# The first 16 rows of a DMA-fed row sum in two transfers, one row and then 15, ahead of the opening barrier

## Chip, cores, metric

One core of one Trainium2 chip. The time is device microseconds (us) of one execution; several executions of each kernel are compared, and the profile is one of them.

## The reference

```python
def reference(x):                      # x: (32, 512, 1024) float32
    relu_x = np.maximum(x, 0)
    return np.sum(relu_x, axis=-1).astype(np.float32)      # (32, 512)
```

16384 rows of 4 KB are read once, 67.1 MB, and 64 KB are written. There is no reuse: the kernel is a stream from HBM with a small sum behind it.

## The kernel before

Each of 128 partitions handles 128 rows. The first 112 rows of a partition come in seven chunks of 16 rows (8 MB, 64 KB contiguous per partition) into three buffers; the last 16 rows come in ever smaller transfers. ScalarE applies the relu in place and VectorE sums; in the last chunk and the tail each engine does whole rows by itself. The opening barrier is the place at the program's start where the engines wait for one another; a load that SyncE issues ahead of it goes out at 0.00 us. Where packets are spoken of, "engine" means one of the 16 DMA engines, and in the profile SPq is SyncE issuing a transfer.

```python
REGIONS = [112, 16]
CHUNKS = [(0, 0), (0, 16), (0, 32), (0, 48), (0, 64), (0, 80), (0, 96)]
ACT_STEPS = [[7, 9], [7, 9], [4, 5, 7], [4, 5, 7], [4, 5, 7], [3, 4, 5]]
DVE_STEPS = [[7, 9], [7, 4, 5], [4, 5, 7], [4, 5, 7], [4, 5, 7], [3, 4, 5]]
TAIL = [8, 4, 2, 1]
# ... (cut)
    code = nc.main_func.blocks[0].instructions
    arrival = next(i for i, ins in enumerate(code)      # SyncE's arrival at the opening barrier
        if ins.engine == mybir.EngineType.SP and type(ins).__name__ == "InstDrain")
    for c in range(NBIG + 1):
        if c >= NB:
            sp.wait_ge(s_dve, done[c - NB])             # buffer free
        if c < NBIG:
            g, j = CHUNKS[c]
            sp.dma_start(out=buf[:, c % NB, :, :],
                         in_=xv[g][:, j : j + BIG, :]).then_inc(s_in[c], 16)
        if c == 0:
            code.insert(arrival, code.pop())            # the first load goes ahead of the barrier
# ... (cut: tail loads, stores)
    for c in range(NTWO):
        act.wait_ge(s_in[c], 16)
        for n in ACT_STEPS[c]:
            t = buf[:, c % NB, r : r + n, :]
            act.activation(t, t, AF.Relu).then_inc(s_act, 1)
        for n in DVE_STEPS[c]:
            # ... wait for s_act
            dve.tensor_reduce(out=res[...], in_=buf[:, c % NB, r : r + n, :],
                              axis=X, op=ALU.add).then_inc(s_dve, 1)
# ... (cut: last chunk, tail, closing store)
```

Of the kernel before, what the change touches and what calls it, by code (L numbers as in the profile page):

```python
# [5 lines left out]
BIG = 16  # L6
NB = 3
REGIONS = [112, 16]
CHUNKS = [(0, 0), (0, 16), (0, 32), (0, 48), (0, 64), (0, 80), (0, 96)]
ACT_STEPS = [[7, 9], [7, 9], [4, 5, 7], [4, 5, 7], [4, 5, 7], [3, 4, 5]]  # L10
DVE_STEPS = [[7, 9], [7, 4, 5], [4, 5, 7], [4, 5, 7], [4, 5, 7], [3, 4, 5]]
TAIL = [8, 4, 2, 1]
# [3 lines left out]
def bass_relu_sum_kernel(  # L16
# [17 lines left out]
    J = B * S // P  # L34
    NBIG = len(CHUNKS)
    assert BIG * NBIG + sum(TAIL) + 1 == J == sum(REGIONS) and sum(LAST) == D
# [4 lines left out]
    xv = [  # L41
        xr[P * s : P * (s + n), :].rearrange("(p j) d -> p j d", p=P)
        for s, n in zip(start, REGIONS)
    ]
    ov = [of[P * s : P * (s + n)].rearrange("(p j) -> p j", p=P) for s, n in zip(start, REGIONS)]

    buf = nc.alloc_sbuf_tensor("buf", [P, NB, BIG, D], fp32)
# [5 lines left out]
    s_in = [nc.alloc_semaphore(f"s_in{i}") for i in range(n_in)]  # L53
# [10 lines left out]
    sp, act, dve = nc.sync, nc.scalar, nc.vector  # L64
# [8 lines left out]
    code = nc.main_func.blocks[0].instructions  # L73
    arrival = next(
        i
        for i, ins in enumerate(code)
        if ins.engine == mybir.EngineType.SP and type(ins).__name__ == "InstDrain"
    )
    for c in range(NBIG + 1):
        if c >= NB:  # L80
            sp.wait_ge(s_dve, done[c - NB])
        if c < NBIG:
            g, j = CHUNKS[c]
            sp.dma_start(out=buf[:, c % NB, :, :], in_=xv[g][:, j : j + BIG, :]).then_inc(
                s_in[c], 16
            )
        if c == 0:
            code.insert(arrival, code.pop())
    r = 0
    tail = []  # L90
    for i, n in enumerate(TAIL):
# [13 lines left out]
    for g in range(len(REGIONS) - 1):  # L105
        sp.dma_start(
            out=ov[g][:, :], in_=res[:, start[g] : start[g] + REGIONS[g]]
# [3 lines left out]
    def on_act(t, acc):  # L111
        return act.activation(t, t, AF.Relu, accum_out=acc)  # L112

    def on_dve(t, acc):
        return dve.tensor_scalar(  # L115
            out=t, in0=t, scalar1=0.0, scalar2=None, op0=ALU.max, op1=ALU.add, accum_out=acc
        )

    def row(c, i):
        return buf[:, c % NB, i, :], res[:, c * BIG + i : c * BIG + i + 1]  # L120

    k = 0
    for c in range(NTWO):
        alone = BIG - sum(ACT_STEPS[c])
        act.wait_ge(s_in[c], 16)
        r = 0
        ready = []
        for n in ACT_STEPS[c]:
            t = buf[:, c % NB, r : r + n, :]
            act.activation(t, t, AF.Relu).then_inc(s_act, 1)  # L130
            k += 1
            ready += [k] * n
            r += n
        for i in range(BIG - alone // 2, BIG):
            on_act(*row(c, i))
        if alone:
            dve.wait_ge(s_in[c], 16)
            for i in range(BIG - alone, BIG - alone // 2):
                on_dve(*row(c, i))
        r = seen = 0  # L140
        for n in DVE_STEPS[c]:
            if ready[r + n - 1] > seen:
                seen = ready[r + n - 1]
                dve.wait_ge(s_act, seen)
            dve.tensor_reduce(  # L145
                out=res[:, c * BIG + r : c * BIG + r + n],
                in_=buf[:, c % NB, r : r + n, :],
                axis=X,
                op=ALU.add,
            ).then_inc(s_dve, 1)  # L150
            r += n
# [1 line left out]

    j0 = NBIG * BIG
    for c in range(NTWO, NBIG):
        act.wait_ge(s_in[c], 16)
        dve.wait_ge(s_in[c], 16)
        for i in range(BIG):
            ins = (on_act if i % 2 else on_dve)(*row(c, i))
            if i >= BIG - 2:  # L160
                ins.then_inc(s_fact if i % 2 else s_fdve, 1)
    for r, n, s in tail[:-1]:
# [13 lines left out]
        out=res[:, j0 + r : j0 + r + 1], in0=half[:, 0:1], in1=half[:, 1:2], op=ALU.add  # L176
    )

    n = LAST[2]
# [41 lines left out]
```

## Time and profile before

| | before |
|---|---|
| time, median of 3 (range) | 161.19 us (161.11 to 161.30) |
| span of the profile | 159.8 us |
| HBM read / written | 67.11 MB / 0.07 MB |
| input queue, share of 16 engines | 98.0% |
| VectorE / ScalarE busy | 121.4 / 101.5 us |
| landing of chunks 1, 2 and of the last input | 21.82, 41.18, 157.75 us |

The landings are the moments at which the last of a transfer's 16 semaphore increments arrives. The prediction below shows the lines that matter. Two things help in reading it. In rate rows and windows a DMA packet counts where it *starts*, with all its bytes, so short windows swing. And the trace keeps a record of each packet (start, duration, size), which shows starts and gaps that no row shows.

### The profile page before, as it was taken

The numbers are of one execution on the slowest core, as the hardware profiler recorded it, in microseconds if no ns is written. First come the engines' busy times: TensorE is split into PE (matmuls) and PEld (weight loads), VectorE is DVE, ScalarE is ACT, GpSimd is POOL, SyncE is SP. The second block draws the span as 40 slices with busy tenths as digits, with TensorE's granted clock in tenths as the row PEclk, the third lists the DMA queues.
The fourth block names the chain that finished last, engine by engine and source line by source line (L and its number), as shares of the span: only waits on it lengthen the run. The fifth ranks groups of instructions, "written<-read, shape, count | busy, mean of one in ns | idle before, by whom it ended". The sixth has DMA issues, their size and how long they took to land.

```text
span 159.8 us, 148 instructions
## 1 busy us (share of the span) xinstructions
DVE 121.4 (76%) x58; ACT 101.5 (63%) x55; POOL 0.2 (0%) x4
## 2 busy tenths in 40 slices
DVE  0000000999959999999969989699899999598995
ACT  3000059990699808996099951999339980496974
POOL 0000000000000000000000000000000000000000
DMA  7996996996997998989969969969969969899994
GB/s 262 525 525 262 525 525 262 525 525 262 525 443 344 525 410 377 525 361 427 525 295 492 525 279 509 525 262 525 525 262 525 525 262 525 353 435 394 406 393 138
DMA packets 2305, 67.18 MB, mean 420 GB/s; under 512 B 512, under 2 KB 768, under 8 KB 1024
## 3 DMA queue, kind: packets, MB, share of 16 engines
q1 hardware_dynamic: 2304, 67.18, 98.0%
q14 instruction: 1, 0.01, 0.0%
HBM read 67.11 MB, written 0.07 MB: 420 GB/s over the span
## 4 chain that ended last, share of the span: by engine, by line
DMA 68%; ACT 18%; DVE 11%; SPq 1%; issue 0%
DMA buf<-in_x_dram 68%; ACT buf L130 18%; DVE res L145 11%; SPq L92 1%; SPq L100 0%; DVE buf L115 0%; DVE last L115 0%
## 5 line engine op out<-in xcount | busy, mean ns | idle before, releaser
L145 DVE TENSOR_REDUCE res<-buf 128x7 f32<-128x7168 f32 (+4 forms) x17 | 100.1, 5923 | 34.0 <-ACT buf L130 34.0
L130 ACT ACTIVATE buf<-buf 128x7168 f32<-128x7168 f32 (+4 forms) x16 | 80.7, 5099 | 46.5 <-DMA buf<-in_x_dram 46.5
L112 ACT ACTIVATE buf<-buf 128x1024 f32<-128x1024 f32 (+1 forms) x19 | 19.0, 1000 | 9.0 <-DMA buf<-in_x_dram 8.9
L115 DVE TENSOR_SCALAR_CACHE_REDUCE buf<-buf 128x1024 f32<-128x1024 f32 (+2 forms) x19 | 20.9, 1146 | 2.8 <-DMA buf<-in_x_dram 2.5
L112 ACT ACTIVATION_READ_ACCUMULATOR buf<-buf 128x1 f32 x19 | 3.5, 186 | 0.0
L130 ACT ACT_TABLE_LOAD x1 | 1.3, 1283 | 0.8 <-PEq L206 0.8
L115 DVE DVE_READ_ACCUMULATOR buf<-buf 128x1 f32 x19 | 1.6, 83 | 0.0
L115 DVE TENSOR_SCALAR_CACHE_REDUCE last<-last 128x258 f32<-128x258 f32 x1 | 0.4, 422 | 0.0
L175 DVE TENSOR_TENSOR res<-half 128x1 f32<-128x1 f32 x1 | 0.2, 160 | 0.1
L206 POOL MEMSET const-bfloat16-1.0<- 128x1 bf16 x1 | 0.1, 101 | 0.0
L206 POOL MEMSET const-uint8-127<- 128x1 uint8 x1 | 0.1, 101 | 0.0
L206 POOL MEMSET const-float32-0.0<- 128x1 f32 x1 | 0.1, 98 | 0.2 <-issue 0.2
L206 POOL MEMSET const-float32-1.0<- 128x1 f32 x1 | 0.1, 98 | 0.0
L115 DVE DVE_READ_ACCUMULATOR last<-last 128x1 f32 x1 | 0.1, 81 | 0.0
## 6 DMA issues: line engine op xcount, KB each, us to landing
buf<-in_x_dram SPq DMA_DIRECT2D x1, 4096.0 KB, 26.7
buf<-in_x_dram SPq DMA_DIRECT2D x1, 2048.0 KB, 31.2
buf<-in_x_dram SPq DMA_DIRECT2D x1, 1024.0 KB, 33.2
buf<-in_x_dram SPq DMA_DIRECT2D x1, 512.0 KB, 34.0
buf<-in_x_dram SPq DMA_DIRECT2D x1, 256.0 KB, 34.2
buf<-in_x_dram SPq DMA_DIRECT2D x1, 128.0 KB, 34.1
last<-in_x_dram SPq DMA_DIRECT2D x1, 128.0 KB, 34.0
buf<-in_x_dram SPq DMA_DIRECT2D x7, 36.3
```

The lines of the kernel that those rows point to most:

```text
L92: sp.dma_start(out=buf[:, tb, r : r + n, :], in_=xv[-1][:, r : r + n, :]).then_inc(s_in[NBIG + i], 16)
L112: return act.activation(t, t, AF.Relu, accum_out=acc)
L115: return dve.tensor_scalar(out=t, in0=t, scalar1=0.0, scalar2=None, op0=ALU.max, op1=ALU.add, accum_out=acc)
L130: act.activation(t, t, AF.Relu).then_inc(s_act, 1)
L145: dve.tensor_reduce(out=res[:, c * BIG + r : c * BIG + r + n], in_=buf[:, c % NB, r : r + n, :], axis=X, op=ALU.add,).then_inc(s_dve, 1)
L175: dve.tensor_tensor(out=res[:, j0 + r : j0 + r + 1], in0=half[:, 0:1], in1=half[:, 1:2], op=ALU.add)
L206: nc = _bacc.Bacc("TRN2", target_bir_lowering=False, num_devices=1)
```

## The change

The intent is to let the stream start with small packets, so that the DMA engines have data flowing sooner, and to have the bulk queued right behind them. Both transfers count on one semaphore, and the waits ask for the sum of 32.

```diff
-CHUNKS = [(0, 0), (0, 16), (0, 32), (0, 48), (0, 64), (0, 80), (0, 96)]
+CHUNKS = [[(0, 0, 1), (0, 1, 15)]] + [[(0, 16 * c + 16, 16)] for c in range(6)]
@@
-            g, j = CHUNKS[c]
-            sp.dma_start(out=buf[:, c % NB, :, :], in_=xv[g][:, j : j + BIG, :]).then_inc(
-                s_in[c], 16
-            )
-        if c == 0:
-            code.insert(arrival, code.pop())
+            i = 0
+            for g, j, n in CHUNKS[c]:
+                sp.dma_start(
+                    out=buf[:, c % NB, i : i + n, :], in_=xv[g][:, j : j + n, :]
+                ).then_inc(s_in[c], 16)
+                i += n
+                if c == 0:
+                    code.insert(arrival, code.pop())
+                    arrival += 1
@@ every wait for a chunk, on ScalarE and VectorE
-        act.wait_ge(s_in[c], 16)
+        act.wait_ge(s_in[c], 16 * len(CHUNKS[c]))
```

More of the change, by code (lines that the diff above doesn't have):

```diff
@@ L136, in bass_relu_sum_kernel @@
         if alone:
-            dve.wait_ge(s_in[c], 16)
+            dve.wait_ge(s_in[c], 16 * len(CHUNKS[c]))
             for i in range(BIG - alone, BIG - alone // 2):
@@ L155, in bass_relu_sum_kernel @@
     for c in range(NTWO, NBIG):
-        act.wait_ge(s_in[c], 16)
-        dve.wait_ge(s_in[c], 16)
+        act.wait_ge(s_in[c], 16 * len(CHUNKS[c]))
+        dve.wait_ge(s_in[c], 16 * len(CHUNKS[c]))
         for i in range(BIG):
```

## The prediction

> **What bounds the kernel now.** I read the page first, then the waits, the SyncE queue's own waits, the timeline of the start and the end, and last the trace's record of single DMA packets. From the page:
>
> ```profile
> span 159.8 us, 148 instructions
> DVE 121.4 (76%) x58; ACT 101.5 (63%) x55; POOL 0.2 (0%) x4
> ...
> DVE  0000000999959999999969989699899999598995
> ACT  3000059990699808996099951999339980496974
> ...
> GB/s 262 525 525 262 525 525 262 525 525 262 525 443 344 525 410 377 525 361 427 525 295 492 525 279 509 525 262 525 525 262 525 525 262 525 353 435 394 406 393 138
> ...
> q1 hardware_dynamic: 2304, 67.18, 98.0%
> ...
> DMA 68%; ACT 18%; DVE 11%; SPq 1%; issue 0%
> ```
>
> No compute engine is full, and the one input queue is busy for 98% of 16 engines' span. The swing of the rate row between 262 and 525 is not a stall. A slice is 4 us and a packet counts where it starts. The packet records show 896 packets of 65536 B, each 2.418 us long and starting 2.416 us after the one before it on its engine, so a slice catches one or two starts per engine (16 x 65536 B / 4.0 us = 262 GB/s). The true rate is 16 x 65536 B / 2.416 us = 434 GB/s, with no hole from the second packet of an engine to the tail.
>
> The waits say who is short of what:
>
> ```profile
> ACT buf L130 <- DMA buf<-in_x_dram: 46.5, 6, 19.8
> DVE res L145 <- ACT buf L130: 34.0, 8, 28.1
> ...
> SPq L84 <- DVE res L145: 99.0, 4, 44.0
> ```
>
> ScalarE waits for a landing before each of the six pipelined chunks. VectorE in turn waits for ScalarE, mostly while nothing has arrived. SyncE waits 99.0 us for buffers, which looks like a bound; the timeline shows it isn't:
>
> ```profile
> 0.00 1.60 SPq L84 DMA_DIRECT2D buf<-in_x_dram  x3
> ...
> 0.79 1.28 ACT L130 ACT_TABLE_LOAD   x1 [0.79 <-PEq L206]
> 21.84 13.95 ACT L130 ACTIVATE buf<-buf 128x7168 f32<-128x7168 f32 x2 [19.77 <-DMA buf<-in_x_dram]
> ...
> 35.82 9.75 DVE L145 TENSOR_REDUCE res<-buf 128x9 f32<-128x9216 f32 x1 [0.15 <-ACT buf L130]
> 41.20 13.95 ACT L130 ACTIVATE buf<-buf 128x7168 f32<-128x7168 f32 x2 [5.41 <-DMA buf<-in_x_dram]
> 45.60 0.33 SPq L84 DMA_DIRECT2D buf<-in_x_dram  x1
> ```
>
> VectorE frees the first buffer at 35.82 + 9.75 = 45.57 us and the fourth chunk is issued at 45.60. The third chunk's packets run to about 60 us, so that issue is some 14 us early. Chunks land every 19.36 us (21.84 to 41.20), that is 8 packets x 2.416 = 19.33 us and 0.03 us for the change of transfer. So the end is set by three things in a row: when the stream starts, 64 rows of 64 KB per engine at 2.416 us (154.6 us), and what follows the last input. The last part is fixed:
>
> ```profile
> 157.88 0.42 DVE L115 TENSOR_SCALAR_CACHE_REDUCE last<-last 128x258 f32<-128x258 f32 x1
> ...
> 158.33 0.34 SPq L190 DMA_DIRECT2D out_dram<-res  x1
> ```
>
> The last input is there at 157.8, the store is issued at 158.33 and lands 1.4 us later, at the end of the span.
>
> The change touches only the first term. There the packet records show: issue at 0.00, first packets of the 16 engines starting between 1.00 and 1.86, ending between 4.07 and 4.53, so 2.6 to 3.5 us long (mean 3.08) in place of 2.42. Counted back from the ends by one full packet, the stream began to flow at 4.07 - 2.42 = 1.65 to 4.53 - 2.42 = 2.11 us. An engine keeps its place to the end, so the slowest engine's 2.11 us is the whole stake of this change, less the issue-to-first-packet time that no splitting removes.
>
> **What the Trainium skill says.** (1) "DMA: Bandwidth & Descriptors", section "Where 436 GB/s comes from", gives a ceiling of 435.2 GB/s for the 16 ports; the trace's 434 agrees, so nothing can make up for a late start. (2) The same page, "Latency and other measured facts", gives about 0.6 us to the first byte for a transfer issued from SyncE and a round trip to HBM of at least about 0.8 us, whatever the size. The trace has 0.84 us from the issue of the closing store to its first packet, and 1.00 us for the first load; both fit a cost that doesn't depend on size. (3) "Perfetto Trace Analysis", section "DMA Optimizations", says that splitting transfers "may allow some to start sooner", if DMA engines are generally idle. Here they are idle only in the first microsecond; after it the trace shows none of that idleness. (4) "DMA: Bandwidth & Descriptors", "Why a DMA increments its semaphore by 16 and not by 1", warns against a wait for the first of two transfers on one semaphore. The new waits are for 32, the sum of both, so they are safe, and they also mean that no engine starts on row 0 early. No run has tested that warning yet.
>
> **The change part by part.**
>
> *Removed:* the first transfer with 8 packets of 64 KB per engine. *Added:* a transfer with 8 packets of 4 KB and one with 8 packets of 60 KB. The bytes are the same, and each row of a partition is one contiguous run in both, so the number of packets for the first 16 rows goes from 128 to 256.
>
> Cost of small packets: the tail's one-row transfer has 4 KB packets of 156 to 159 ns that follow each other after about 155 ns, against 2416/16 = 151 ns for 4 KB within a large packet. 8 x 4 ns = 0.03 us. One more change of transfer costs 0.03 us as above. Sum +0.06 us on the path. Some two dozen of the tail's 128 packets of 4 KB were longer, 168 to 421 ns; the one-row transfer landed 1.3 us after the two-row one (155.02 to 156.32) where 1.21 us of data are due. So a further 0 to 0.1 us.
>
> SyncE's second issue: the issues of line 84 last 0.33 to 0.42 us. SyncE reaches the barrier about 0.38 us later, and since the second chunk is now issued at 0.79, right after the barrier, it goes out at about 1.2. It is not needed before the first 16 rows have been read, at about 21 us: no cost. The ScalarE table load moves from 0.79 to about 1.2 and ends at 2.5, against data at 21.8: no cost. Are the 60 KB packets there in time? Their issue follows the first by 0.4 us, so they should be ready at 1.4 to 2.3 us, while the 4 KB packets occupy an engine for 1.24 us from its first byte. No hole if flow starts at 1.65 or later; a hole of a few tenths at most if it starts at 1.0.
>
> Gain: only what the small first packets save out of the ramp. If the ramp is pure latency (issue, descriptors, first answer from HBM), the gain is 0. If a 64 KB packet itself makes the ramp longer, as by 16 engines asking for a megabyte at once, the gain is at most the mean 3.08 - 2.42 = 0.66 us, or for the slowest engine 2.11 - 1.0 = 1.1 us. I weigh these as about 3 to 1 for latency and take the expected gain as 0.25 x 0.7 = 0.17 us. With +0.06 to +0.1 of cost the sum is -0.1 us: 161.19 - 0.1 = 161.1.
>
> **Rivals.** *The first packets flow sooner.* For it: an engine whose first packet is recorded at 1.00 needs 3.52 us for it, but the one recorded last, at 1.86, needs only 2.62. So the early ones were held by something shared, not by their own distance to HBM, and less to fetch at once might free them. Against: all 16 end within 0.46 us whatever their start, as if all had waited for the same first answer. It would make 160.4 to 160.8. *The 4 KB packets stumble.* For it: the tail's long ones of up to 421 ns. Eight hops from one partition's rows to the next, 112 rows of 4 KB or 448 KB further on, right at the start, with all engines in step, could meet this at each hop, 8 x 0.05 to 0.1 us. Against: the tail loses only 0.1 us in its one-row transfer. It would make 161.4 to 161.9. *The later barrier becomes the bound:* it would need the second chunk to be 20 us late; it is 0.4 us late. It would make 161.19. *ScalarE becomes the bound:* it would start chunk 0 later than its landing; nothing it does before takes more than 2.5 us.
>
> **Range and chances.** The mechanism's whole stake is below 1.2 us either way, and 2% is 3.2 us. A gain of 3.2 us would need data before the issue; a loss of 3.2 us would need the 8 small packets to cost 0.4 us more each, more than the worst seen in the tail. The before runs lie within 0.2 us. So 161.1, range 160.5 to 161.7, and nearly all the chance within 2%.
>
> **What would show it.** In the changed kernel's profile the first slice of the rate row changes, since 4 KB packets start there, and the queue has 128 data packets more and 16 semaphore packets. ScalarE's first chunk should start at 21.84 within -0.6 and +0.3 us, and every later landing and the end should shift by the same amount, with the 19.36 us spacing unchanged. ScalarE's table load should stand at about 1.2. If the first landing shifts but the end doesn't, my claim that nothing after the start has slack in the stream is wrong. If the 60 KB packets last other than 2.416 x 15/16 = 2.265 us, the rate is not what I took it for. If the 4 KB packets show gaps before the first 60 KB packet, the second issue comes too late.

## The result, and the profile after

| | before | after |
|---|---|---|
| time, median of 6 (before: the three runs above and three more) | 161.15 us (161.09 to 161.30) | 161.17 us (161.08 to 161.27) |
| ratio after / before, 95% interval | | 1.000 (0.9987 to 1.0013) |
| span of the profile | 159.80 us | 159.76 us |
| landing of chunks 1, 2 and of the last input | 21.82, 41.18, 157.75 | 21.79, 41.15, 157.64 |

Ratios are the mean time of one kernel's runs over that of the other's of the same rounds, so not quite the ratio of the medians quoted. The change does nothing to the time that these runs can show; the interval is about 0.2 us to either side.

Page of the changed kernel; the rows are as in the page before (the rate row is GB/s in 40 slices, the queue row has packets, MB and share):

```profile
span 159.8 us, 149 instructions
...
GB/s 377 492 323 415 492 525 263 525 525 263 525 476 312 525 427 361 525 394 394 525 312 476 525 279 509 525 263 525 525 263 525 509 279 525 353 435 390 416 404 122
...
q1 hardware_dynamic: 2448, 67.18, 98.0%
...
DMA 68%; ACT 18%; DVE 11%; SPq 1%; issue 0%
```

The first slice reads 377 in place of 262 GB/s. That isn't a faster start: the sixteen 64 KB packets that began in that slice before are now 4 KB and 60 KB packets, more of which begin in it. The queue has 2448 - 2304 = 144 packets more, which is 128 of data and 16 semaphore increments. The chain is unchanged.

Timeline of the changed kernel's start (start, duration, engine, line, instruction, idle time before and its releaser):

```profile
0.00 2.25 SPq L85 DMA_DIRECT2D buf<-in_x_dram  x4
...
1.27 1.28 ACT L133 ACT_TABLE_LOAD   x1 [1.27 <-PEq L209]
21.81 13.95 ACT L133 ACTIVATE buf<-buf 128x7168 f32<-128x7168 f32 x2 [19.26 <-DMA buf<-in_x_dram]
...
35.79 9.75 DVE L148 TENSOR_REDUCE res<-buf 128x9 f32<-128x9216 f32 x1 [0.15 <-ACT buf L133]
```

SyncE issues the first four loads at 0.00, 0.43, 1.27 and 1.65 us (records of the single issues); before, the second chunk went out at 0.79. The barrier opens 0.48 us later, which moves the table load from 0.79 to 1.27. ScalarE's first chunk starts at 21.81 in place of 21.84 us, and the chunks after it land 0.02 to 0.04 us earlier. The closing computation too:

```profile
157.84 0.42 DVE L118 TENSOR_SCALAR_CACHE_REDUCE last<-last 128x258 f32<-128x258 f32 x1
...
158.29 0.34 SPq L193 DMA_DIRECT2D out_dram<-res  x1
```

Both lines stand 0.04 us earlier than before. What the start gives, the end gets; but 0.03 us between one profile of each kernel is no finding, since runs of one kernel lie 0.2 us apart.

What happens in the first microseconds is seen in narrow windows (window, length, busy times, clock, DMA share, GB/s). First the kernel before, then the changed one:

```profile
0.00:1.00 1.00, 0.00 (x0) 0.21 (x1) 0.20 (x4) 1.00 0.00 0
1.00:2.00 1.00, 0.00 (x0) 1.00 (x1) 0.00 (x0) 1.00 3.09 1049
2.00:3.00 1.00, 0.00 (x0) 0.07 (x1) 0.00 (x0) 1.00 0.00 0
```

```profile
0.00:1.00 1.00, 0.00 (x0) 0.00 (x0) 0.20 (x4) 1.00 0.00 0
1.00:2.00 1.00, 0.00 (x0) 0.73 (x1) 0.00 (x0) 1.00 0.95 168
2.00:3.00 1.00, 0.00 (x0) 0.55 (x1) 0.00 (x0) 1.00 2.12 885
```

The 1049 GB/s before is 16 packets of 64 KB that began in that microsecond and ended at 4.07 us or later. With 4 KB packets the window becomes a meter: 41 of them began in the second microsecond, 168 GB/s, less than 40% of the 434 that the stream runs at later. Both kernels have no packet before 1.0 us.

The packet records of the changed kernel give the rest. The engines' first packets start at 1.01 us at the earliest, as before (1.00). An engine's eight 4 KB packets are over between 2.82 and 3.31 us, though at the later pitch of 155 ns they would need 1.24 us. The time is lost mostly in 26 of the 128, which last 0.18 to 1.06 us and all start by 2.30 us; each of the 65 that start later takes 0.16 us. The first 60 KB packet follows the semaphore increment within some 10 ns on every engine, and lasts 2.267 us.

A measure that is free of packet sizes: take the moment at which an engine starts its first packet of the second chunk, and count back eight packets of 64 KB (8 x 2.416 = 19.33 us). This is when a stream without any ramp would have had to start. I call it the engine's *effective start*. It is read some 21 us into the run, so it holds all that was lost until then. Before, its mean over the 16 engines is 1.91 us and that of the slowest engine 2.11 us; after, 1.83 and 2.10 us. The mean moved by 0.08 us, the slowest engine by 0.01.

### The profile page after: what moved, and what is told of

Read it like the earlier page. It is cut to its first block, busy times and chain, and to the rows that moved or that the text cites. A ratio compares the mean times of both kernels' runs of the same rounds, so it can differ in the third digit from the quotient of the medians.

```text
span 159.8 us, 149 instructions
## 1 busy us (share of the span) xinstructions
DVE 121.4 (76%) x58; ACT 101.5 (64%) x55; POOL 0.2 (0%) x4
## 3 DMA queue, kind: packets, MB, share of 16 engines
q1 hardware_dynamic: 2448, 67.18, 98.0%
## 4 chain that ended last, share of the span: by engine, by line
DMA 68%; ACT 18%; DVE 11%; SPq 1%; issue 0%
DMA buf<-in_x_dram 68%; ACT buf L133 18%; DVE res L148 11%; SPq L95 1%; SPq L103 0%; DVE last L118 0%; DVE buf L118 0%
```

## The experiments

Twelve runs were made, of eleven kernels (one was run again), each against the kernel before on the same chip, in three groups of four (three chips). All gave correct results. Diffs are against the changed kernel.

The theory to begin with was the prediction's: the end is the start of the stream plus a fixed length, and the start is latency that a smaller first transfer doesn't shorten. Rivals: the start has slack; the size of the first packets matters; the consumers matter.

### Whole chunk, issued after the barrier

```diff
-CHUNKS = [[(0, 0, 1), (0, 1, 15)]] + ...
+CHUNKS = [[(0, 0, 16)]] + ...
-                if c == 0:
+                if False:
                     code.insert(arrival, code.pop())
```

> The first 16 rows in one transfer as in the kernel before, but issued after the opening barrier. Theory (the end is the start of the load stream plus a fixed length): SyncE reaches the barrier at once and issues at 0.4 to 0.8 us, so the stream and every landing move later by that, and the time is 161.5 to 161.95 us, 0.4 to 0.8 above the kernel before. Rival (the first landing has slack because the compute engines wait for each other): 161.15 us. If the theory holds, the two kernels compared had a start worth moving, and the change did not move it.

Measured: 161.94 us (161.72 to 161.99) against 161.19, ratio 1.0040 (1.0027 to 1.0053). Timeline:

```profile
0.73 1.33 SPq L85 DMA_DIRECT2D buf<-in_x_dram  x3
22.65 13.95 ACT L133 ACTIVATE buf<-buf 128x7168 f32<-128x7168 f32 x2 [20.64 <-DMA buf<-in_x_dram]
```

The issue is 0.73 us later, the first chunk 0.81 us, the end of the span 0.84 us. The start has no slack. The place ahead of the barrier is worth 0.75 us, and both kernels that are compared already have it.

### The 15 rows after the barrier

```diff
-                if c == 0:
+                if c == 0 and i == 1:
                     code.insert(arrival, code.pop())
```

> The changed kernel, with only the one-row transfer ahead of the barrier; the 15 rows are issued after it, at about 0.8 us in place of 0.43. Theory: the one row keeps every DMA engine busy until 2.8 to 3.3 us, and packets of a second transfer are ready 1.0 to 1.9 us after its issue, so at 1.8 to 2.7; no hole opens, and the time stays within 0.1 us of 161.15. Rival (the second transfer's lead ahead of the barrier is what keeps the split from costing something): a hole of 0.37 us, 161.5 us.

Measured: 160.97 us against 161.19; runs 160.90, 160.85, 161.39, 163.14, 161.03, 160.84; ratio 1.0010 (0.9972 to 1.0048). No hole opened: row 0 was over at 2.64 to 2.94 us, earlier than in the changed kernel (2.82 to 3.31), and the 60 KB packets followed at once although issued at 0.78. So the second transfer needn't be ahead of the barrier. But four of six runs lay below every run of the kernel before, and 163.14 made the interval wide. This was more than the theory allowed for, and a second theory came of it: that the bytes asked for at 0.43 crowd the first row's answers. It was tested further down.

### The 15 rows late

```diff
+    s_late = nc.alloc_semaphore("s_late")
+    late = nc.alloc_sbuf_tensor("late", [P, 2048], fp32)
@@
             for g, j, n in CHUNKS[c]:
+                if c == 0 and i == 1:
+                    sp.wait_ge(s_late, 1)
@@
-                if c == 0:
+                if c == 0 and i == 1:
                     code.insert(arrival, code.pop())
@@
+    dve.memset(late[:, :], 0.0).then_inc(s_late, 1)
```

> The changed kernel, with the 15 rows held back until VectorE has filled a tile of 2048 columns that nothing uses; issue expected at 2 to 3.5 us. Theory: a transfer flows to the slowest engine 2.1 us after its issue, and the one row ends at 3.3, so each tenth of a us by which the issue is later than 1.2 us is a hole and comes out at the end one to one: an issue at t gives 161.15 + (t - 1.2), that is 162.0 to 163.5. Rival (a start later by one or two us is taken up somewhere in 155 us of stream, or an engine with a full queue catches up): within 0.3 us of 161.15.

Measured: 163.02 us (162.89 to 163.25) against 161.19, ratio 1.0114 (1.0101 to 1.0127). Timeline:

```profile
1.28 1.76 DVE L129 MEMSET late<- 128x2048 f32 x1 [1.28 <-PEq L214]
23.51 13.95 ACT L138 ACTIVATE buf<-buf 128x7168 f32<-128x7168 f32 x2 [21.45 <-DMA buf<-in_x_dram]
```

The fill ended at 3.04, the issue came at 3.07 us (record of the issue). The formula gives 161.15 + (3.07 - 1.2) = 163.02 us. That it agrees to the hundredth is luck, as the runs lie 0.36 us apart. What is shown: the slowest engine's effective start is 1.73 us later than in the changed kernel, and the time is 1.83 us above the kernel before, so a hole at the start isn't taken up later. That a second transfer may be issued up to about 1.2 us at no cost isn't shown; issues at 0.43 and 0.79 cost nothing that shows, the one at 3.07 did. The packet records add something: row 0 was over at 3.03 us at the latest, the 60 KB packets began between 4.03 and 4.66, and the first of each engine took 2.56 to 3.17 us in place of 2.267. The late transfer met slow first packets of its own.

### Sixteen single rows

```diff
-CHUNKS = [[(0, 0, 1), (0, 1, 15)]] + ...
+CHUNKS = [[(0, j, 1) for j in range(16)]] + ...
```

> The first 16 rows in 16 transfers of one row, all ahead of the barrier. It multiplies the cost of the split that the prediction put at 0.03 us for eight 4 KB packets and 0.03 us for one more transfer. Theory: 16 x 8 x 4 ns = 0.5 us for the packets and 15 x 0.03 = 0.45 us for the transfers, so 162.1 us (161.9 to 162.3), with the first chunk landing at 22.7; the 16 issues end at about 7 us and delay ScalarE's table load, at no cost. Rival (small packets at the start cost nothing, as the changed kernel's end suggests): 161.2. Rival (each transfer's packets stumble on a first answer): 8 x 0.1 us a row and more, over 163 us.

Measured: 162.79 us (162.13 to 163.05) against 161.19, ratio 1.0096 (1.0080 to 1.0111). The windows of this kernel show the ramp best, since all packets of the stretch are small:

```profile
1.00:1.50 0.50, 0.00 (x0) 0.00 (x0) 0.00 (x0) 1.00 1.02 188
1.50:2.00 0.50, 0.00 (x0) 0.00 (x0) 0.00 (x0) 1.00 0.86 270
2.00:3.00 1.00, 0.00 (x0) 0.00 (x0) 0.00 (x0) 1.00 0.96 381
3.00:4.00 1.00, 0.00 (x0) 0.00 (x0) 0.00 (x0) 1.00 1.09 410
4.00:5.00 1.00, 0.00 (x0) 0.00 (x0) 0.00 (x0) 1.00 0.82 324
...
12.00:16.00 4.00, 0.00 (x0) 0.00 (x0) 0.00 (x0) 1.00 1.02 417
```

The first packet starts at 1.0 us, and 16 engines need two more microseconds to come up to the rate of small packets, about 410 GB/s. That is a ramp, not only a delay. The landings of rows 3 to 15 on the slowest engine go from 6.95 to 22.40 us, 1.29 us for each of 12 rows, against 1.21 at full rate: 0.08 us for one row as a transfer of its own, where I had 0.06. The rest, which I hadn't expected, is one stumble: between the second and the third row's landing 2.21 us pass on the slowest engine, and the spread of the engines grows from 0.51 to 1.34 us and stays. The window from 4 to 5 us shows the dip. So the ordinary cost was about right, and the stumble put five of the six runs above the expected range.

### A wait of its own for the one row

```diff
-ACT_STEPS = [[7, 9], ...      -DVE_STEPS = [[7, 9], ...
+ACT_STEPS = [[1, 6, 9], ...   +DVE_STEPS = [[1, 6, 9], ...
-                ).then_inc(s_in[c], 16)
+                ).then_inc(s_row if c == 0 and i == 0 else s_in[c], 16)
@@ ScalarE
-        act.wait_ge(s_in[c], 16 * len(CHUNKS[c]))
+        if c == 0:
+            act.wait_ge(s_row, 16)
+        else:
+            act.wait_ge(s_in[c], 16)
@@ after the first row's relu
+            if c == 0 and r == 1:
+                act.wait_ge(s_in[c], 16)
```

> The changed kernel, with a semaphore of its own for the one row, so that ScalarE and VectorE start on it when it lands (3.7 us) in place of waiting for all 16 rows (21.8 us). Theory: the compute engines wait for every landing as it is, so an earlier start on one row gives nothing: within 0.1 us of 161.15 although ScalarE is then done with the first chunk about a us earlier. Rival (the split would have paid if the wait had been split too): up to 1 us less, 160.2.

Measured: 161.23 us (161.13 to 161.28) against 161.15, ratio 1.0000 (0.9988 to 1.0012). Timeline:

```profile
3.68 1.06 ACT L137 ACTIVATE buf<-buf 128x1024 f32<-128x1024 f32 x1 [1.15 <-DMA buf<-in_x_dram]
...
21.79 13.10 ACT L137 ACTIVATE buf<-buf 128x6144 f32<-128x6144 f32 x2 [17.05 <-DMA buf<-in_x_dram]
...
41.14 6.18 ACT L137 ACTIVATE buf<-buf 128x7168 f32<-128x7168 f32 x1 [6.25 <-DMA buf<-in_x_dram]
```

ScalarE works on row 0 eighteen microseconds earlier, is done with the chunk 0.87 us sooner (34.89 in place of 35.76), and then waits longer for the next landing, 6.25 us in place of 5.41. The consumers don't bind here, so the missing separate wait is not why the split gave nothing.

### A quarter of a row first

```diff
-                sp.dma_start(out=buf[:, c % NB, i : i + n, :], in_=xv[g][:, j : j + n, :])
+                if c == 0:     # each partition's 64 KB as one run: 1 KB, then 63 KB
+                    lo, hi = (0, D // 4) if i == 0 else (D // 4, BIG * D)
+                    o = buf[:, 0, :, :].rearrange("p j d -> p (j d)")[:, lo:hi]
+                    s = xv[0][:, 0:BIG, :].rearrange("p j d -> p (j d)")[:, lo:hi]
+                # ... else as before
+                sp.dma_start(out=o, in_=s)
```

> The first transfer is a quarter of a row (1 KB packets), the second the other 63 KB of each partition's 64, both ahead of the barrier. Theory (a start that is pure latency): the small transfer is over at 1.65 + 8 x 0.042 = 2.0 to 2.45 us, and the second one's packets could flow at 0.43 + 1.65 = 2.1 to 0.43 + 2.11 = 2.5, so a hole of up to 0.1 us: 161.15 to 161.35. Rival (less asked for at once makes the first answer come sooner): 160.5 to 160.9. Rival (the ramp that a transfer of large packets meets comes anyway, after the small ones): 161.5 or more.

Measured: 161.62 us (161.31 to 161.82) against 161.15, ratio 1.0023 (1.0011 to 1.0035). Small, but clear of 1. The eight 1 KB packets of an engine were over at 1.43 to 1.74 us, sooner than the 2.0 to 2.45 of my theory: a small first transfer really is there earlier. But it ends before the next transfer can flow. The first 63 KB packets, issued at 0.43, took 2.93 to 3.65 us against 2.38 at full rate: they went through a ramp like that of the first packets before. The mean effective start is 2.14 us, later than the 1.91 of one transfer. This fits the second rival best, that a ramp comes anyway after the small packets. The early flow was nothing that the stream could use.

### Two halves

```diff
-CHUNKS = [[(0, 0, 1), (0, 1, 15)]] + ...
+CHUNKS = [[(0, 0, 8), (0, 8, 8)]] + ...
```

> The first 16 rows in two transfers of 8 rows (32 KB packets), both ahead of the barrier. Theory: the size of the first packets doesn't matter to when the stream starts; the first packets of 32 KB end at 1.65 to 2.11 plus 1.21, so at 2.85 to 3.35 us, and the time is 161.15 to 161.25. Rival (the size of the first packets sets the ramp): between the one-row and the whole-chunk kernel, which are equal, so this can only tell a ramp that both have by accident; over 161.5 or under 160.9 would show one.

Measured: 161.14 us (161.00 to 161.78) against 161.15, ratio 1.0002 (0.9987 to 1.0017). The first 32 KB packets end at 2.84 to 3.30 us, as predicted, and the effective start is 1.85 us in the mean and 2.12 on the slowest engine. With first packets of 4, 32 and 64 KB the slowest engine starts at 2.10, 2.12 and 2.11 us. As one kernel's effective start differed by 0.22 us between two chips (the table below), the hundredths are chance; that there is no difference of 0.3 us or more rests on the ratio, against the kernel before on the same chip.

### The 15 rows from ScalarE's queue

```diff
-                sp.dma_start(
+                (act if c == 0 and i == 1 else sp).dma_start(
@@ the place ahead of the barrier is ScalarE's own for this one
```

> The changed kernel, with the 15 rows issued by ScalarE ahead of the barrier, at the same time as SyncE's one row. Theory: both transfers meet the same latency; the stream starts no sooner than with one issuer, the packets of the two queues interleave on each engine, the one row lands later than 3.7 us, and the time is within 0.15 us of 161.15. Rival (the issues follow each other in one queue, and that holds the first packets back; the spread of their starts between 1.0 and 1.9 us comes from one issuer): the first packets start closer together, and the time falls by 0.3 us or more.

Measured: 163.61, 163.69 and 161.33 us (three more of 163.78 to 164.01 were more than 1.5% above the fastest), against 161.15; ratio 1.0103 (1.0050 to 1.0155). Five of the six lie between 163.61 and 164.01 us. My expectation of 0.15 us was wrong, but not at the start: the first packets start at 1.00 us as ever. Queues and timeline:

```profile
q1 hardware_dynamic: 2304, 59.31, 85.7%
q10 hardware_dynamic: 144, 7.86, 11.2%
```

```profile
34.04 31.30 ACT L137 ACTIVATE buf<-buf 128x7168 f32<-128x7168 f32 x5 [31.84 <-DMA buf<-in_x_dram]
```

With two queues, the engines take turns between the 15 rows and the second chunk, and the first chunk is complete at 34.0 in place of 21.8 us. Its buffer is free 12 us later, the fourth chunk is issued at 57.8 in place of 45.6 us, and of the packets that start between 60 and 64 us most take 2.5 to 3.4 us in place of 2.42. In the prediction I counted 14 us of slack for that issue; this run used 12 of them, the queue wasn't empty at 57.8 (the third chunk landed at 60.6), and time was lost all the same. Why the packets are slow there is open; one run of six escaped it. It says nothing on the split itself, except that in five runs of six the two transfers did better in one queue.

### The crowding theory: four kernels more

*The 15 rows after the barrier, again* (same diff as above):

> The run with the 15 rows after the barrier once more, because its five close runs lay 0.15 to 0.35 us under the kernel before, but one of 163.14 us made the interval too wide. Crowding theory, formed since (a first packet is answered later when more bytes have been asked of HBM at the same time): with the 15 rows issued at 0.78 in place of 0.43, row 0 is over on the slowest engine at 2.95 us in place of 3.3, and the median is 160.85 to 161.05. Pure latency: 161.1 to 161.2, and the first showing was chance.

Measured on another chip: 161.07 us (160.96 to 161.22) against 161.16, ratio 0.9992 (0.9979 to 1.0006). Row 0 was over at 2.80 to 3.30 us, as in the changed kernel, with the second issue at 0.79.

*Two single rows ahead, and one ahead with one after:*

```diff
-CHUNKS = [[(0, 0, 1), (0, 1, 15)]] + ...
+CHUNKS = [[(0, 0, 1), (0, 1, 1), (0, 2, 14)]] + ...
-                if c == 0:
+                if c == 0 and i <= 2:      # second kernel: i == 1
                     code.insert(arrival, code.pop())
```

> Transfers of 1, 1 and 14 rows, the two single rows ahead of the barrier, the 14 after it. The second issue is as early as in the changed kernel, but asks for a fifteenth of the bytes. Crowding by bytes: row 0 is over at 2.95 us as with the rest after the barrier, the second row at about 4.2, and the time is 160.9 to 161.1. Crowding by the issue itself (the descriptors of a second transfer hold back the first one's): row 0 over at 3.3 us, 161.2. Pure latency: 161.2, with one more split.

> Transfers of 1, 1 and 14 rows, one ahead of the barrier and the others after it, so that the large transfer is issued at about 1.2 us. Crowding by bytes: row 0 over at 2.9 us or sooner, two rows at 4.15, and the time 160.85 to 161.05, no better than the rest after the barrier, as row 0 was already alone there. If an even later large transfer helps: under 160.8. Pure latency: 161.2.

Measured: 162.06 us (161.98 to 162.34), ratio 1.0056 (1.0043 to 1.0069), and 162.00 us (161.89 to 162.28), ratio 1.0053 (1.0040 to 1.0065), against 161.16. No theory had this. Timeline of the first of them:

```profile
22.75 13.95 ACT L133 ACTIVATE buf<-buf 128x7168 f32<-128x7168 f32 x2 [20.21 <-DMA buf<-in_x_dram]
```

Two engines of 16 are slow in their first 56 KB packet (3.10 and 3.11 us in place of 2.116), a third in part (2.50); in the second kernel three engines enter it late (4.70 to 5.05 us, the others by 4.47) and are slow in it (2.27 to 2.85). The slowest engine's effective start is 3.05 and 3.09 us, with a mean of 2.20 and 2.21. The transfer ends with its slowest engine. It looks like the stumble of the sixteen rows, which came at the same time and after two single rows too. Its cause is open.

*One, three and twelve rows:*

```diff
-CHUNKS = [[(0, 0, 1), (0, 1, 15)]] + ...
+CHUNKS = [[(0, 0, 1), (0, 1, 3), (0, 4, 12)]] + ...
-                if c == 0:
+                if c == 0 and i == 1:
                     code.insert(arrival, code.pop())
```

> Transfers of 1, 3 and 12 rows, one ahead of the barrier, growing in steps. Crowding by bytes: at most a tenth under the one with 15 rows after the barrier, 160.8 to 161.0; the step from small to large packets meets less. Pure latency: 161.2.

Measured: 161.15 us (161.04 to 161.33) against 161.16, ratio 0.9998 (0.9985 to 1.0010). Three transfers alone don't bring the stumble. All three kernels with two single rows one after the other had it in their profiles, and each of their runs is slower than every run of the kernel before in its group.

The crowding theory is not borne out. It gave row 0 over at 2.95 us and 160.85 to 161.05 us for the repeated run, and got 3.30 and 161.07. The bytes that had fully arrived by 2.0 us, from the packet records, with the time of the second issue:

| kernel | chip group | second issue, us | KB arrived by 2.0 us |
|---|---|---|---|
| 15 rows after the barrier | first | 0.78 | 160 |
| 15 rows late | first | 3.07 | 172 |
| sixteen single rows | first | 0.43 | 160 |
| own wait for the row | second | 0.42 | 76 |
| 15 rows after the barrier, again | third | 0.79 | 72 |
| two single rows ahead | third | 0.42 | 80 |
| second row after | third | 0.78 | 100 |
| one, three, twelve | third | 0.79 | 100 |
| changed kernel | its own | 0.43 | 100 |

Within a group the bytes don't go with the time of the second issue, whether it comes at 0.43 or 3.07 us. The groups differ. Whether the ramp differs from chip to chip or from one session to the next, the runs don't tell.

### All runs in one table

Effective start, as defined above, against the span of the profiled run, all in us:

| kernel | effective start, mean | slowest engine | span | span less slowest |
|---|---|---|---|---|
| before | 1.91 | 2.11 | 159.80 | 157.69 |
| changed | 1.83 | 2.10 | 159.76 | 157.66 |
| whole chunk after the barrier | 2.61 | 2.94 | 160.65 | 157.71 |
| 15 rows after the barrier, first / again | 1.65 / 1.82 | 1.87 / 2.09 | 159.54 / 159.73 | 157.67 / 157.64 |
| 15 rows late | 3.64 | 3.83 | 161.64 | 157.81 |
| sixteen single rows | 3.03 | 3.99 | 161.69 | 157.70 |
| own wait for the row | 1.82 | 2.10 | 159.72 | 157.62 |
| quarter row first | 2.14 | 2.72 | 160.30 | 157.58 |
| two halves | 1.85 | 2.12 | 159.76 | 157.64 |
| two single rows ahead | 2.20 | 3.05 | 160.99 | 157.94 |
| second row after | 2.21 | 3.09 | 160.65 | 157.56 |
| one, three, twelve | 1.79 | 1.96 | 159.69 | 157.73 |

Thirteen profiles obey one rule within 0.25 us (the run with two queues, which loses its time elsewhere, is left out): the span is the slowest engine's effective start plus 157.7 us. A change to the first transfer is worth what it does to that one engine, and not to the mean: for the two single rows ahead the mean would give 2.20 + 157.89 (what before has) = 160.1 us, and the span is 160.99. As the start is read at 21 us, the rule says that nothing is won or lost after it; why an engine starts late it doesn't say. One profile stands for each kernel, so differences under 0.25 us can't be read from it.

## Why the prediction was right

It gave 161.1 us, 160.5 to 161.7, with nearly all the chance within 2%; 161.17 was measured, and the ratio is 1.000. That the number fits is no test of its gain and its cost: each was under 0.2 us, and the runs resolve 0.2. That both came out near nothing is in part luck. The mechanism was tested by the experiments.

- *The stream binds, and a shift at the start comes out at the end:* shown. The whole chunk after the barrier, issued 0.73 us later, took 0.75 us more; the 15 rows late took 1.83 us more, for an effective start 1.73 us later; an earlier consumer moved nothing. The three terms of the prediction don't make up the span, though: 2.11 + 154.6 + 2.05 us (157.75 to 159.80) is 158.8 of 159.8. About half of the missing 1.0 us lies in the tail, whose 16 rows take 19.8 us in place of 19.33. Both kernels have it, so the comparison doesn't suffer.
- *Nothing else comes onto the path:* shown. The table load moved by 0.48 us (I said about 0.4), the second chunk's issue to 1.27 us, no hole opened before the 60 KB packets, and their 2.267 us is the predicted 2.265.
- *Cost of the split, 0.06 us:* shown in size by the sixteen rows, 0.08 us for each. The further "0 to 0.1 us" for stumbling packets was too little as a general bound: where a second single row follows the first, two or three engines fall behind, the slowest by about 1 us. The change, with its one row, doesn't meet it.
- *Gain, 0 with a weight of 3 in 4, else about 0.7 us:* the size came out as in the first case, but its reason was too simple. I called it pure latency. The runs show a ramp: the first packets start at 1.0 us, and the core's rate climbs from below 200 to above 400 GB/s over two microseconds. The rival's ground, that something shared holds the early engines, isn't ruled out; its conclusion, that smaller first packets would free them, didn't come true. With packets of 4, 32 and 64 KB the time is the same. A transfer of 1 KB packets is through sooner, and the large packets behind it then meet a ramp of their own. What makes the ramp is open. (The mean of the first 64 KB packets is 3.09 us and not 3.08; nothing hangs on it.)
- *The total of -0.1 us:* measured +0.02 in the medians, and -0.04 in the profiled runs. Neither differs from zero, and neither tells the prediction's -0.1 from the +0.06 to +0.1 that its pure latency would have made.

The 15 rows after the barrier are the one version that may be faster than both, 160.97 and 161.07 us in two groups against 161.19 and 161.16. Both intervals contain 1, so I don't claim it; the medians differ by 0.14% and 0.06%.

## What to carry to other kernels

Where a load stream is never interrupted, measure a change to its first transfer by one number, the moment at which the slowest DMA engine would have had to start at full rate; here earlier first landings and earlier work on them were worth nothing by themselves. Moving the issue itself counted in full (0.75 us for the place ahead of the barrier). Cutting the first transfer into pieces won nothing that the runs show in any of the cuts tried: with first packets of 4, 32 and 64 KB alike the slowest engine counted from 2.1 us. Small pieces in front can do harm out of proportion (0.8 us or more for a second single row), as an engine that stumbles once is late to the end.

## What the Trainium skill lacked or had wrong

- "DMA: Bandwidth & Descriptors", section "Latency and other measured facts", has a time to the first byte, about 0.6 us, and none for the ramp after it. Here the first packet's record began 1.00 us after the issue of the first load and 0.84 us after that of the closing store. In the kernel of sixteen single rows 188, 270, 381 and 410 GB/s followed in the windows from 1.0 to 4.0 us, and the mean engine's stream counted from 1.8 to 1.9 us after the issue, in the changed kernel and the one before.
- "Perfetto Trace Analysis", section "DMA Optimizations", says that splitting may let some transfers start sooner, and that the whole task may end sooner if the DMA engines are generally idle (the prediction ties this condition to the start). It doesn't say what a split costs where they are busy. Here one row split off changed the time by a ratio of 1.000, a quarter of a row cost 0.2%, and two single rows cost 0.5 to 0.6%.
- "DMA: Bandwidth & Descriptors", section "Anatomy of one DMA — SWDGE (gpsimd) path", gives a fixed cost of about 2.0 us per transfer for its path. For loads queued behind each other from SyncE, these runs show 0.08 us for each single-row transfer of 512 KB more; the page has the rate of such a stream, but no cost per transfer.
- The same page, section "Issuing engines are not separate DMA queues", says that transfers from different issuers interleave and that a second issuer saves only issue time. The run agrees that they interleave, and has a cost that the section leaves out: the older of two transfers was complete at 34.0 in place of 21.8 us.
- No page has the stumble of two or three engines, up to 1 us each, after two transfers of 4 KB packets at the start of a stream; its cause is open.
